# Grouped-query attention: Exp over three PSUM banks, one bank each for VectorE's scores and for outputs, chains of three cells

## The chip, the core and the metric

The kernel runs on one core of one Trainium2 chip. The metric is device time in microseconds. The core has these engines: TensorE (PE in the profile; PEld is its weight load), VectorE (DVE), ScalarE (ACT), GpSimd (POOL) and SyncE (SP, here only a DMA queue). Each engine runs its own instruction stream in order, and semaphores make one stream wait for another. TensorE writes its results into PSUM, which has eight banks of 128 partitions by 512 fp32 numbers.

## The reference

```
batch, n_q_heads, n_kv_heads, seq, head_dim = (8, 8, 2, 1024, 64)
...
scale = 1.0 / np.sqrt(head_dim)
for g in range(n_kv_heads):
    ...
    scores = scale * np.matmul(q_group, k_group.transpose(0, 1, 3, 2))
    scores_max = np.max(scores, axis=-1, keepdims=True)
    attn = np.exp(scores - scores_max)
    attn = attn / (np.sum(attn, axis=-1, keepdims=True) + 1e-08)
    output[:, q_start:q_end, :, :] = np.matmul(attn, v_group)
```

The inputs are fp32, normal numbers times 0.1. Four query heads share one key and value head. The kernel computes in bf16 and leaves the maximum out.

## The kernel before

**Jobs and cells.** A job is one batch, one query head and one half of its 1024 queries: 8 x 8 x 2 = 128 jobs. A job has eight cells, one for each 128 keys. A cell is one score matmul: 128 keys on the partitions by 512 queries, in one PSUM bank (`score`, L466). So there are 1024 cells.

**Two ways to the exponential.** An A cell goes to ScalarE: cells are gathered in a PSUM tile of two banks (`aps`, two such tiles), and one ACTIVATE with Exp (`exps`, L477) turns the whole tile into bf16 in a ring in SBUF (`p_ring`). A D cell goes to VectorE: its score lies in one of two single banks (`dps`), and VectorE makes from it the bits of a bf16 power of two (`exp_bits`, L491, called p1 below). Ten such cells form a group `pd`, and a chain of four instructions over the group corrects the mantissa: "and" (L512, VectorE), "line" (L516, GpSimd, the linear factor), "prod" (L525, VectorE) and "add" (L527, VectorE).

**Outputs.** For each cell, four small matmuls (`output_mms`, L538, called a PV below) multiply the exponentials by V, which has a column of ones, so the sum of the exponentials comes with it. The eight PVs of one job add up in one PSUM bank (`ops`; there are two). Then `normalise` takes the reciprocal of the sum (L551) and multiplies (L554), both on VectorE, into a staging tile, from where a DMA writes the result. The first PV of a job that takes an output bank (it "opens" the bank) must wait until the job before in that bank has been normalised.

**PSUM.** 2 tiles x 2 banks for Exp, 2 banks for VectorE's scores, 2 for outputs: eight in all.

**The order of the work** is written by a planner, `make_plan`. It steps through the kernel with a clock for each engine and a cost for each operation, takes at each step the operation that could start soonest, and notes its time. The notes, sorted by time, are the order in which the instructions are issued on every engine (`tc.manual_schedule`, L617); semaphores still enforce the real dependences. The planner's costs and limits are the constants of L34 to L42. An output bank is chosen in an event of its own:

```
            at = max(pe, FIRST_PV, min(obank_free), at)
...
        elif kind == "open":
            o = first_free(obank_free)
            obank[arg] = o
            obank_free[o] = INF
```

and the PVs of the job are noted afterwards at `max(pe, FIRST_PV, ready...)` (L94).

**Data.** Q and K are cast to bf16 through a DRAM scratch by GpSimd's DMA queue (L323) and brought back transposed by SyncE's (L335); V comes by GpSimd's queue (L356). A cast is made to wait for the latest score matmul planned before it (L329), as a brake. GpSimd's DMA issues stand in the same stream as its "line" instructions; `at_pool` moves an issue behind a "line" if it would fall shortly before it.

Of the kernel before, what the change touches and what calls it, by code (L numbers as in the profile page):

```python
# [11 lines left out]

CURVE_A, CURVE_B = 0.32988085, -0.33401025

A_CELLS, D_BANKS, O_BANKS = (2, 2), 2, 2
GROUP, PARTS = 10, 2
CHAIN = ("and", "line", "prod", "add")
ON_POOL = ("line",)

def part(step, m):  # L20

    n = step[-1]
    return slice(0, m) if not n.isdigit() else slice(m * int(n) // PARTS, m * (int(n) + 1) // PARTS)


def make_plan(nj, nkc):
# [6 lines left out]

    QK, PV, P1, NORM = 0.216, 0.1225, 0.603, 0.555  # L34
    EXP = (0.05, 0.4268)
    FOUR, TWO, POOL_ONE = (0.09, 0.133), (0.05, 0.27), (0.25, 0.43)
    COST = {"and": FOUR, "line": POOL_ONE, "prod": TWO, "add": TWO}
    FROM_PE, FROM_PV, FROM_ACT, FROM_DVE, FROM_POOL = 0.21, 0.16, 0.165, 0.10, 0.15
    LIVE_A, LIVE_D, PENDING, PER_JOB, LEAD, RAMP, AHEAD, FIRST_PV = 28, 5, 16, 2, 6, 6, 0.0, 2.0
    INF = 1e9  # L40
    AHEAD_D, EXTRA, LAST = 0, 0, 6
    FIRST_TURN, FIRST_LOAD, EACH_LOAD = 2.4, 4.5, 4.2  # L42
    ops = []
    pe = act = dve = pool = two_end = 0.0
# [7 lines left out]
    p1q, chainq, normq, cur = [], [], [], []  # L52
# [10 lines left out]
    def first_free(slots):  # L63
        return min(range(len(slots)), key=lambda s: slots[s])


    while normed < nj:
# [46 lines left out]
        if kind == "qk":  # L114
            t = best[4]
            pe = t + QK
            j = job_d if arg else job_a
            cell = j * nkc + todo[j].pop(0)
            if not arg:
                if open_a is None:  # L120
                    slot = first_free(a_free)
                    a_id += 1
                    live["A"] += 1
                    open_a = {"slot": slot, "t": a_free[slot], "cells": []}
                    a_free[slot] = INF
                o = open_a
                ops.append((t, "qk", cell, "A", a_id, o["slot"], len(o["cells"])))
                o["cells"].append(cell)
                home[cell] = ("A", a_id)
                if len(o["cells"]) == A_CELLS[o["slot"]] or not any(todo[job_a:]):  # L130
                    act = max(act, pe + FROM_PE)
                    ops.append((act, "exp", a_id, tuple(o["cells"])))
                    act += EXP[0] + EXP[1] * len(o["cells"])
                    a_free[o["slot"]] = act + FROM_ACT
                    uses[("A", a_id)] = len(o["cells"])
                    for x in o["cells"]:
                        ready[x] = act + FROM_ACT
                    open_a = None
            else:
                taken[j] += 1  # L140
                k = first_free(bank)
                bank[k] = INF
                pending += 1
                ops.append((t, "qk", cell, "D", k, 0, 0))
                p1q.append((pe + FROM_PE, cell, k))
# [4 lines that stand above are left out]
            open_jobs.append(arg)  # L150
            rem[arg] = list(range(nkc))
            next_job += 1
        elif kind == "pv":
            s, c = arg
            cell = s * nkc + c
            opens = len(rem[s]) == nkc
            rem[s].remove(c)
            done = not rem[s]
            ops.append((t, "pv", s, cell, opens, done, obank[s]))
            pe = t + PV  # L160
            h = home[cell]
            uses[h] -= 1
            if not uses[h]:
                live[h[0]] -= 1
            if done:
                open_jobs.remove(s)
                normq.append((pe + FROM_PV, s))
        elif kind == "norm":
            s = normq.pop(0)[1]
            ops.append((t, "norm", s))  # L170
            dve = t + NORM
            obank_free[obank[s]] = dve + FROM_DVE
            normed += 1
        elif kind == "p1":
            _, cell, k = p1q.pop(0)
            if not cur:
                d_id += 1
                live["D"] += 1
            ops.append((t, "p1", cell, k, d_id, len(cur)))
            dve = t + P1  # L180
            bank[k] = dve + FROM_DVE
            cur.append(cell)
            home[cell] = ("D", d_id)
            if len(cur) == GROUP:
                chainq.append((dve, d_id, cur, 0))
                cur = []
        elif kind == "flush":
            chainq.append((dve, d_id, cur, 0))
            cur = []
        else:  # L190
            _, g, cells, step = chainq.pop(arg)
            ops.append((t, "chain", g, len(cells), CHAIN[step]))
            name = CHAIN[step]
            fixed, each = COST[name.rstrip("0123456789")]
            end = t + fixed + each * len(cells[part(name, len(cells))])
            if name in ON_POOL:
                pool = end
            else:
                dve = two_end = end
            if step + 1 < len(CHAIN):  # L200
                at = end
                if (name in ON_POOL) != (CHAIN[step + 1] in ON_POOL):
                    at += FROM_POOL if name in ON_POOL else FROM_DVE
                chainq.insert(arg, (at, g, cells, step + 1))
            else:
                pending -= len(cells)
                uses[("D", g)] = len(cells)
                for x in cells:
                    ready[x] = dve + FROM_DVE
# [4 lines left out]
def kernel(  # L214
# [8 lines left out]
    FP32 = mybir.dt.float32  # L223
    BF16 = mybir.dt.bfloat16
# [12 lines left out]
    QBS = 512  # L237
    HALF = S // 2
# [3 lines left out]
    PIECE = 512  # L242
    WARM = 30
    CAST_GAP = 3.0
    P_TILES = 28
    POOL_DMA = 1.0
    OBSERVE = 26
    scale = 1.0 / math.sqrt(D)
    bits_scale = 128.0 * scale * math.log2(math.e)
    bits_bias = 128.0 * 127.0  # L250
# [13 lines left out]
    const_pool = ctx.enter_context(tc.tile_pool(name="constp", bufs=1))  # L264
# [3 lines left out]
    first_pool = ctx.enter_context(tc.tile_pool(name="firstp", bufs=1))  # L268
    qT_pool = ctx.enter_context(tc.tile_pool(name="qTpool", bufs=10))
    kT_pool = ctx.enter_context(tc.tile_pool(name="kTpool", bufs=4))  # L270
    pd_pool = ctx.enter_context(tc.tile_pool(name="pdpool", bufs=5))
    tmp_pool = ctx.enter_context(tc.tile_pool(name="tmppool", bufs=2))
    ostage_pool = ctx.enter_context(tc.tile_pool(name="ostage", bufs=6))
    recip_pool = ctx.enter_context(tc.tile_pool(name="recip", bufs=10))
# [1 line left out]
    def psum_pools(name, n):  # L276
        return [
            ctx.enter_context(
                tc.tile_pool(name=f"{name}{i}", bufs=1, space=bass.MemoryType.PSUM)
            )  # L280
            for i in range(n)
        ]

    apools, dbanks, obanks = psum_pools("aps", 2), psum_pools("dps", 2), psum_pools("ops", 2)

    p_ring = const_pool.tile([128, P_TILES, 2, QBS], BF16)
    blank = const_pool.tile([128, 128], BF16)
    nc.vector.memset(blank, 1.0)  # L288
    ident = const_pool.tile([128, 128], BF16)
# [75 lines left out]
    def first_loads():  # L365
# [5 lines left out]

        hk = first_pool.tile([128, NHC, 3, D], BF16, name="hk")

        tk = [
            dbanks[0].tile([128, HALF], BF16, name="dps0"),
            apools[1].tile([128, HALF], BF16, name="aps1"),
        ]
        lo, hi = slice(0, D), slice(D, 2 * D)

        def turn_k(w, half, bank):  # L380
# [21 lines left out]
        for two in range(2):  # L402
            place_v(0, 0, two)

        warm = obanks[1].tile([128, 128], FP32, name="ops1")

        def keep_warm(n):
            for _ in range(n):
# [1 line left out]
            return mm.ins  # L410

        hq = first_pool.tile([128, NHC, 2 * D], BF16, name="hq")
        tq = [
            dbanks[1].tile([128, HALF], BF16, name="dps1"),
            obanks[0].tile([128, HALF], BF16, name="ops0"),
        ]
        qT[(0, 0)] = qT_pool.tile([128, HALF], BF16, name="qT")
        last_score[0] = keep_warm(WARM)
        for n, half in enumerate(halves):
# [30 lines left out]
    psum = {}  # L450
# [6 lines left out]
    def score(cell, kind, n, slot, col):  # L457
        b, h, side = jobs[cell // NKC]
        c = cell % NKC
        if kind == "A":  # L460
            if col == 0:
                psum[("A", n)] = apools[slot].tile([128, 2, QBS], FP32, name=f"aps{slot}")
            dst = psum[("A", n)][:, col, :]
        else:
            dst = psum[cell] = dbanks[n].tile([128, QBS], FP32, name=f"dps{n}")
        last_score[0] = nc.tensor.matmul(  # L466
            dst,
            lhsT=ksets[b % 2][:, h // HPG, side, c * 128 : (c + 1) * 128],
            rhs=qT[(b, h)],
            start=True,  # L470
            stop=True,
        ).ins

    def exps(n, cells):
        pt = p_ring[:, n % P_TILES]
        m = len(cells)
# [4 lines left out]
        exp_ins.append(act.ins)  # L481
        if n >= P_TILES and (n - P_TILES) % OBSERVE == 0:
            seen = exp_ins[n - P_TILES + OBSERVE - 1]
            tc.add_manual_dep(act.ins, seen.name, SYNC, reason="ring")
# [101 lines left out]
    for b in range(B):  # L586
        for h in range(H):
# [3 lines left out]
            spare = min(1.0, max(0.0, th - 12.0) / 60.0)  # L591
# [59 lines left out]
```

The softmax here doesn't subtract the row's maximum and nothing guards it: scores larger than these inputs give would overflow.

## Time and profile before

| | |
|---|---|
| median of 3 runs | 385.43 us (385.39 to 386.04) |
| the profiled execution | 385.81 us |
| its span, first to last instruction | 384.0 us |
| TensorE clock granted | 1.00 of full speed nearly throughout, 0.998 in the mean |
| ACTIVATE with Exp | 404, of two banks each |
| cells on ScalarE / VectorE | 808 / 216 |
| chains | 21 of ten cells, one of six |

An instruction's time in the profile runs from its start to its end; on VectorE and ScalarE the next one may start a little before the end of the last. So the cost of an instruction in a full engine is best read from start to start, and an engine that reads as 100% busy may still lose some hundredths of a microsecond at each instruction. In the table of waits each line has the engine and line that waited, who released it, the total wait in us, how often, and the longest. In the timeline each line has the start, the length, the engine, the source line, the operation, out<-in and how many were merged; an idle time before it and its releaser may stand in brackets.

### The profile page before, as it was taken

What the parts mean: (1) busy time and instruction counts of PE and PEld (TensorE: products, weight loads), DVE (VectorE), ACT (ScalarE), POOL (GpSimd) and SP (SyncE); (2) the same over time, 40 slices, a digit from 0 to 9 for tenths busy, and PEclk for the clock granted to TensorE, in tenths of its full rate; (3) what the DMA queues carried; (4) which work ended last, traced back from release to release, by engine and by line L of the source; (5) the groups of instructions that cost most, each with busy time, mean ns of one, the idle gap of its engine ahead of it and who ended that gap; (6) DMA issues with size and microseconds to landing.
All of it is one profiled execution on the core that took longest, in us unless ns stands there. A gap on an engine that the chain in (4) does not pass through costs nothing.

```text
span 384.0 us, 12026 instructions
## 1 busy us (share of the span) xinstructions
PE 365.6 (95%) x5172; PEld 233.6 (61%) x5172; DVE 353.8 (92%) x548; ACT 374.6 (98%) x409; POOL 174.4 (45%) x147
## 2 busy tenths in 40 slices
PE   8879898999999999999999999999999999998995
PEld 7425464666666666666666666666666666564664
DVE  4779998999999999999999999999999999989982
ACT  5999999999999999999999999999999999999995
POOL 5584535718244371563718245271643627040420
PEclk9999999999999999999999999999999999999999
DMA  8988988697756848585676759468675765711213
GB/s 137 135 152 135 130 154 124 129 147 140 113 109 132 140 103 139 101 156 103 139 131 120 130 106 152 96 126 137 105 124 123 138 102 119 126 56 29 57 56 84
DMA packets 102485, 45.48 MB, mean 118 GB/s; under 512 B 63792, under 2 KB 100976, under 8 KB 101184
## 3 DMA queue, kind: packets, MB, share of 16 engines
q1 hardware_dynamic: 82096, 31.21, 36.1%
q0 software_dynamic: 19712, 13.18, 32.3%
q8 instruction: 40, 0.66, 0.7%
q10 hardware_dynamic: 624, 0.33, 0.3%
q14 instruction: 13, 0.11, 0.1%
HBM read 25.17 MB, written 27.00 MB: 136 GB/s over the span
## 4 chain that ended last, share of the span: by engine, by line
ACT 86%; PE 10%; DVE 2%; issue 1%
ACT p_ring L477 86%; PE aps L466 4%; PE ops L538 4%; PE ops L409 1%; PE dps L466 1%; DVE pd L527 1%; DVE ost L554 0%; DVE y L525 0%; DVE z L512 0%; DVE rec L551 0%; PE dps L382 0%; PE dps L428 0%; PE ops L428 0%; PE aps L382 0%; DVE blank L288 0%
## 5 line engine op out<-in xcount | busy, mean ns | idle before, releaser
L477 ACT ACTIVATE p_ring<-aps 128x1024 bf16<-128x1024 f32 x404 | 371.8, 1067 | 1.4 <-PE aps L466 1.2
L466 PE MATMUL aps<-qT,kset 128*128 128x512 bf16 x808 | 239.9, 378 | 13.0 <-ACT p_ring L477 12.4
L538 PEld LDWEIGHTS <-p_ring 128*128 128x128 bf16 x3232 | 140.1, 98 | 64.0
L538 PE MATMUL ops<-vset,p_ring 128*128 128x65 bf16 x3232 | 154.6, 194 | 0.0
L491 DVE TENSOR_SCALAR pd<-dps 128x512 uint16<-128x512 f32 x216 | 138.6, 683 | 7.0 <-PE dps L466 6.7
L516 POOL TENSOR_SCALAR y<-z 128x5120 f16<-128x5120 uint16 (+1 forms) x22 | 96.4, 4383 | 70.0 <-DVE rec L551 48.7
L466 PEld LDWEIGHTS <-kset 128*128 128x128 bf16 x1024 | 79.7, 97 | 56.4 <-issue 25.8
L323 POOL DMA_DIRECT2D scr_q<-in_q_dram x63 | 39.1, 621 | 83.5 <-PE dps L466 44.3
L466 PE MATMUL dps<-qT,kset 128*128 128x512 bf16 x216 | 76.4, 379 | 0.0
L525 DVE TENSOR_TENSOR y<-z,y 128x5120 f16<-128x5120 uint16 (+1 forms) x22 | 61.0, 2772 | 1.1 <-POOL y L516 1.1
L527 DVE TENSOR_TENSOR pd<-pd,y 128x5120 uint16<-128x5120 uint16 (+1 forms) x22 | 60.9, 2769 | 0.1
L554 DVE TENSOR_TENSOR ost<-ops,rec 128x256 f32<-128x256 f32 x128 | 54.3, 425 | 4.4
L538 PEld LDWEIGHTS <-pd 128*128 128x128 bf16 x864 | 42.8, 98 | 24.7 <-DVE ost L554 2.2
L538 PE MATMUL ops<-vset,pd 128*128 128x65 bf16 x864 | 52.2, 194 | 0.3
L512 DVE TENSOR_SCALAR z<-pd 128x5120 uint16<-128x5120 uint16 (+1 forms) x22 | 32.3, 1467 | 0.5
L551 DVE RECIPROCAL rec<-ops 128x4 f32<-128x4 f32 x128 | 22.6, 176 | 9.6 <-PE ops L538 8.2
L323 POOL DMA_DIRECT2D scr_k<-in_k_dram x15 | 9.8, 656 | 39.9 <-PE aps L466 33.0
L356 POOL DMA_DIRECT2D vset<-in_v_dram x32 | 24.9, 784 | 0.0
L409 PE MATMUL ops<-blank 128*128 128x128 bf16 x40 | 5.3, 313 | 1.1 <-DVE blank L288 1.1
L409 PEld LDWEIGHTS <-blank 128*128 128x128 bf16 x40 | 4.4, 149 | 1.1 <-DVE blank L288 1.1
L363 POOL DMA_DIRECT2D kset<-kset x6 | 4.1, 684 | 0.0
L420 ACT ACT_TABLE_LOAD x1 | 1.3, 1283 | 1.8 <-issue 1.8
(23 smaller groups left out, 10.2 us busy)
## 6 DMA issues: line engine op xcount, KB each, us to landing
out_dram<-ost SPq DMA_DIRECT2D x63, 256.0 KB, 2.9
scr_q<-in_q_dram POOLq DMA_DIRECT2D x63, 128.0 KB, 3.5
kset<-kT SPq DMA_DIRECT2D x60, 64.0 KB, 3.1
vset<-in_v_dram POOLq DMA_DIRECT2D x32, 64.0 KB, 3.9
scr_k<-in_k_dram POOLq DMA_DIRECT2D x15, 128.0 KB, 3.7
qT<-scr_q SPq DMA_TRANSPOSE x63, 3.5
kset<-kset POOLq DMA_DIRECT2D x6, 128.0 KB, 4.3
fq<-in_q_dram ACTq DMA_DIRECT2D x2, 128.0 KB, 3.3
```

Of the source, the lines that this page charges most:

```text
L323: dma = nc.gpsimd.dma_start(out=scr.rearrange("(p f) -> p f", f=1024), in_=src.rearrange("(p s) d -> p (s d)", s=1024 // D),)
L356: nc.gpsimd.dma_start(out=vsets[b % 2][:, g, two * NHC : (two + 1) * NHC, 0:D], in_=v[b, g].rearrange("(c p two) d -> two p c d", p=128, t ...
L466: last_score[0] = nc.tensor.matmul(dst, lhsT=ksets[b % 2][:, h // HPG, side, c * 128 : (c + 1) * 128], rhs=qT[(b, h)], start=True, stop=Tr ...
L477: act = nc.scalar.activation(out=pt[:, 0:m], in_=psum.pop(("A", n))[:, 0:m], func=AF.Exp, scale=scale)
L491: nc.vector.tensor_scalar(out=groups[g][:, slot], in0=psum.pop(cell), scalar1=bits_scale, scalar2=bits_bias, op0=ALU.mult, op1=ALU.add,)
L512: eng.tensor_scalar(out=z, in0=pd, scalar1=0x7F, scalar2=None, op0=ALU.bitwise_and)
L516: eng.tensor_scalar(out=y, in0=z, scalar1=CURVE_A / 128.0, scalar2=CURVE_B, op0=ALU.mult, op1=ALU.add,)
L525: eng.tensor_tensor(out=y, in0=z, in1=y, op=ALU.mult)
L527: eng.tensor_tensor(out=pd, in0=pd, in1=y, op=ALU.add)
L538: nc.tensor.matmul(ops_of[s][:, qs, :], lhsT=p_of[cell][:, qs * 128 : (qs + 1) * 128], rhs=vsets[b % 2][:, h // HPG, c, :], start=opens an ...
L551: nc.vector.reciprocal(out=rec, in_=o[:, :, D])
L554: nc.vector.tensor_tensor(out=stage[(b, h)][:, :, side, :], in0=o[:, :, 0:D], in1=rec.unsqueeze(2).to_broadcast([128, NQS, D]), op=ALU.mult,)
```

## The change

The Exp tiles have three banks instead of two, and there are still two of them: six banks. VectorE's scores have one bank instead of two, and so have the outputs. A chain covers three cells instead of ten. Its "line" stays on GpSimd. The planner's constants change with it. The group tiles `pd` grow in number from 5 to 8, and the ring holds 18 tiles of three cells instead of 28 of two. The first loads use other banks as scratch. The operations that are computed stay the same.

```diff
-A_CELLS, D_BANKS, O_BANKS = (2, 2), 2, 2
-GROUP, PARTS = 10, 2
+A_CELLS, D_BANKS, O_BANKS = (3, 3), 1, 1
+GROUP, PARTS = 3, 2
...
-    FOUR, TWO, POOL_ONE = (0.09, 0.133), (0.05, 0.27), (0.25, 0.43)
+    FOUR, TWO, POOL_ONE = (0.20, 0.133), (0.05, 0.27), (0.25, 0.417)
...
-    FROM_PE, FROM_PV, FROM_ACT, FROM_DVE, FROM_POOL = 0.21, 0.16, 0.165, 0.10, 0.15
-    LIVE_A, LIVE_D, PENDING, PER_JOB, LEAD, RAMP, AHEAD, FIRST_PV = 28, 5, 16, 2, 6, 6, 0.0, 2.0
+    FROM_PE, FROM_PV, FROM_ACT, FROM_DVE, FROM_POOL = 0.21, 0.20, 0.165, 0.135, 0.06
+    LIVE_A, LIVE_D, PENDING, PER_JOB, LEAD, RAMP, AHEAD, FIRST_PV = 18, 8, 6, 2, 2, 6, 0, 2.0
...
-    AHEAD_D, EXTRA, LAST = 0, 0, 6
+    AHEAD_D, EXTRA, LAST = 0.1, 0, 6
...
-                chainq.append((dve, d_id, cur, 0))
+                chainq.append((dve + 0.11, d_id, cur, 0))
...
-    P_TILES = 28
+    P_TILES = 18
...
-    OBSERVE = 26
+    OBSERVE = 16
...
-    pd_pool = ctx.enter_context(tc.tile_pool(name="pdpool", bufs=5))
+    pd_pool = ctx.enter_context(tc.tile_pool(name="pdpool", bufs=8))
...
-    apools, dbanks, obanks = psum_pools("aps", 2), psum_pools("dps", 2), psum_pools("ops", 2)
-
-    p_ring = const_pool.tile([128, P_TILES, 2, QBS], BF16)
+    apools = psum_pools("aps", len(A_CELLS))
+    dbanks, obanks = psum_pools("dps", D_BANKS), psum_pools("ops", O_BANKS)
+
+    p_ring = const_pool.tile([128, P_TILES, max(A_CELLS), QBS], BF16)
...
-        tk = [
-            dbanks[0].tile([128, HALF], BF16, name="dps0"),
-            apools[1].tile([128, HALF], BF16, name="aps1"),
-        ]
+        spare = apools[1].tile([128, A_CELLS[1], 2 * QBS], BF16, name="aps1")
+        tk = [dbanks[0].tile([128, HALF], BF16, name="dps0"), spare[:, 0, :HALF]]
...
-        warm = obanks[1].tile([128, 128], FP32, name="ops1")
+        warm = apools[0].tile([128, 128], FP32, name="aps0")
...
-        tq = [
-            dbanks[1].tile([128, HALF], BF16, name="dps1"),
-            obanks[0].tile([128, HALF], BF16, name="ops0"),
-        ]
+        tq = [spare[:, 1, :HALF], obanks[0].tile([128, HALF], BF16, name="ops0")]
...
-                psum[("A", n)] = apools[slot].tile([128, 2, QBS], FP32, name=f"aps{slot}")
+                psum[("A", n)] = apools[slot].tile(
+                    [128, A_CELLS[slot], QBS], FP32, name=f"aps{slot}"
+                )
```

The order in which the changed kernel issues its instructions can be read without running it. It has 273 ACTIVATEs of three banks and one of one bank (820 A cells), 204 p1 (204 D cells), and 68 chains of three cells. On VectorE the cycle most often repeated is: p1, and, p1, normalise, p1, prod, add, normalise.

More of the change, by code (lines that the diff above doesn't have):

```diff
@@ L184, in make_plan @@
             if len(cur) == GROUP:
-                chainq.append((dve, d_id, cur, 0))
+                chainq.append((dve + 0.11, d_id, cur, 0))
                 cur = []
         elif kind == "flush":
-            chainq.append((dve, d_id, cur, 0))
+            chainq.append((dve + 0.11, d_id, cur, 0))
             cur = []
```

## The prediction

> **What bounds the kernel now.** I read the page first: busy time, then the chain of waits, then the costliest groups.
>
> ```profile
> PE 365.6 (95%) x5172; PEld 233.6 (61%) x5172; DVE 353.8 (92%) x548; ACT 374.6 (98%) x409; POOL 174.4 (45%) x147
> ...
> ACT 86%; PE 10%; DVE 2%; issue 1%
> ...
> L477 ACT ACTIVATE p_ring<-aps 128x1024 bf16<-128x1024 f32 x404 | 371.8, 1067 | 1.4 <-PE aps L466 1.2
> ```
>
> ScalarE carries the end (86% of the chain is Exp), with TensorE and VectorE close behind it. Its 100% hides small losses: by the timeline an Exp starts 0.90 us after the last at best, and the 404 take 372 us from 7.40 to 379.43, which is 0.92 each. So 404 x 0.903 = 364.8 is work and some 7 us are waits of hundredths, for the two-bank tiles. The table of waits shows the same from TensorE's side, and how rarely the output bank matters with two of them:
>
> ```profile
> PE aps L466 <- ACT p_ring L477: 12.4, 40, 0.3
> ...
> PEld L538 <- DVE ost L554: 2.2, 5, 0.6
> ```
>
> One of those five waits, in the timeline at 30 us, gives the price of a normalise for the PV behind it: reciprocal at 30.47, multiply at 30.68, ended at 31.11, next PV at 31.16. So the bank comes back **0.69 us** after the reciprocal starts, and TensorE started no other matmul meanwhile.
>
> ```profile
> 30.47 0.18 DVE L551 RECIPROCAL rec<-ops 128x4 f32<-128x4 f32 x1
> 30.68 0.42 DVE L554 TENSOR_TENSOR ost<-ops,rec 128x256 f32<-128x256 f32 x1
> ...
> 30.51 0.59 PE L466 MATMUL aps<-qT,kset 128*128 128x512 bf16 x2
> 31.16 0.42 PE L538 MATMUL ops<-vset,pd 128*128 128x65 bf16 x8
> ...
> 31.16 0.30 PEld L538 LDWEIGHTS <-pd 128*128 128x128 bf16 x8 [0.55 <-DVE ost L554]
> ```
>
> The score bank's round trip, from the same view: p1 starts at 203.79, the next score in its bank at 204.53 (0.74 later); a score that starts at 7.63 is read by p1 at 8.05 (0.42).
>
> ```profile
> 203.79 0.68 DVE L491 TENSOR_SCALAR pd<-dps 128x512 uint16<-128x512 f32 x1
> ...
> 204.53 0.38 PE L466 MATMUL dps<-qT,kset 128*128 128x512 bf16 x1
> ```
>
> VectorE's costs, start to start, for chains of ten cells and the one of six:
>
> ```profile
> 201.83 1.49 DVE L512 TENSOR_SCALAR z<-pd 128x5120 uint16<-128x5120 uint16 x1
> 203.24 0.17 DVE L551 RECIPROCAL rec<-ops 128x4 f32<-128x4 f32 x1
> ...
> 366.53 0.95 DVE L512 TENSOR_SCALAR z<-pd 128x3072 uint16<-128x3072 uint16 x1
> 367.40 0.18 DVE L551 RECIPROCAL rec<-ops 128x4 f32<-128x4 f32 x1
> ...
> 370.35 1.76 DVE L525 TENSOR_TENSOR y<-z,y 128x3072 f16<-128x3072 uint16 x1
> 372.03 0.18 DVE L551 RECIPROCAL rec<-ops 128x4 f32<-128x4 f32 x1
> ```
>
> "and": 1.41 for ten, 0.87 for six, so 0.135 a cell and 0.06 fixed: 0.465 for three. "prod": 2.74 (207.95 to 210.69) and 1.68, so 0.265 and 0.09: 0.885 for three. "add": 2.74 and 1.66, so 0.86. Where add follows prod at once it starts 2.85 after it (24.28, 27.13), 0.11 more: 0.99. p1 costs 0.60, normalise 0.55 (203.24 to 203.79).
>
> **What the Trainium skill says.** "Perfetto Trace Analysis", section Matmuls: independent matmul groups should rotate through PSUM banks so that reading one out lies beside the next group's matmuls. The trace agrees: with two output banks, 2.2 us of waits in 128 jobs. "TensorE: Matmul & The Clock Gate", section Step-by-step: only weight loads are pulled ahead, "The MATMULs themselves stay in program order". The gap before 31.16 agrees. So a PV that waits holds every score behind it. The same page, section "A second HAM failure mode": short idle times between groups of matmuls can lower the granted clock. Here the clock is 0.998, so the trace does not show it; it serves as a rival. For a price: "ScalarE: Activation LUTs", section "What ACT_TABLE_LOAD costs", gives 0.833 ns an element, so a third bank adds an estimated 512 x 0.833 = 0.427 to 0.903: **1.330** for a three-bank Exp. The trace has only one length; 0.45 at most (half of 0.903, nothing fixed) to 0.41 at least bounds the whole at +7 and -5 us.
>
> **The change part by part.**
> 1. Exp: 273 x 1.330 + 0.48 = 363.6 of issue, 1.2 less than before (131 instructions fewer, twelve A cells more). A two-bank tile has little slack: 1.07 (Exp) + 0.215 (second score) + 0.42 = 1.70 of 1.81. A three-bank one has 1.50 + 0.43 + 0.42 = 2.35 of 2.66, 0.31. So most of the 7 us of small waits could go.
> 2. VectorE: chains 22 x 6.9 less the short one = 149 before; 68 x (0.465 + 0.99 + 0.86) = 157 after; p1 twelve fewer, -7. About +1, beside Exp.
> 3. GpSimd: "line" of three takes 4.46 - 7 x 0.427 = 1.47 (slope from 4.46 and 2.75), in all 100 us of an engine that is half idle. From "and" to "prod": 0.55 + 0.12 + 1.47 + 0.03 = 2.17. Its DMA issues stand behind a line and have over 2 us to the next. Nothing.
> 4. Start: VectorE's first score is now first on TensorE, in the bank that held the turned K, so it waits for the copy at L391 (6.40 + 0.42). First Exp at about 7.9 instead of 7.40.
> 5. One score bank and one output bank. Here I follow the order of issue through the cycle that fills 49 of the 68 chains. Jobs X, Y, Z; time 0 is the reciprocal of X, right behind an add. TensorE: six PVs of Y (the first opens the bank), two A scores, D score b, an A score, two PVs that end Y, two A, D score c, one A, then Z opens. VectorE: normalise X, p1 a, and, p1 b, normalise Y, p1 c, prod, add, normalise Z.
>    - Y's first PV: 0.69 (the one bank). Six PVs are 24 matmuls at 0.031: 0.74. Two A scores at 0.215: 0.43. D score b at 1.86, p1 b at 1.86 + 0.42 = 2.28. VectorE alone would be there at 0.55 + 0.60 + 0.465 = 1.61, so it stands idle for 0.67.
>    - Normalise Y at 2.88; p1 c at 3.43 (by VectorE 2.88 + 0.55, by the bank 2.28 + 0.74 + 0.42, equal); prod at 4.04 (line done at 1.15 + 2.17 = 3.32, in time); add 5.03; normalise Z at **5.89**.
>
>    The cycle closes at 5.89 although no engine has that much work: VectorE 5.22, ScalarE 4 x 1.330 = 5.32, TensorE 15 x 0.215 + 16 x 0.124 = 5.21. It is a loop: normalise, output bank, PVs, score, p1, normalise, p1, chain, normalise. With two output banks the PVs of Y would not wait. The planner misses it: the event that takes a bank knows when it is free, but the PVs are noted at TensorE's own clock, so scores meant for ScalarE and VectorE are placed behind a PV that stalls.
>    - So Exp loses 5.89 - 5.32 = 0.57 in each such cycle: 49 x 0.57 = 27.9. The other 19 chains have more scores between jobs. Following one such stretch the same way, three chains (one of the common kind, two others) take 16.49 against 3 x 5.32 = 15.96, so only the common one loses; the one after it has five PVs in front and loses 0.12 less (-0.7 over six places). 27.2.
>
> Sum: 7.9 + 363.6 + 27.2 + 1.5 for the first chains and small waits (I take 1.5 from 0 to 4) + 4.7 from the last Exp's issue to the span's end, as now (379.43 to 384.0, and 0.1 of overlap) = 404.9. The profiled execution has 1.8 outside its span and lies 0.4 above the median: **406.3**.
>
> **Rivals.**
> - *The loop is looser.* If a normalise finds its PVs earlier than I think, or slack carried from the other chains covers 0.3 of each 0.57, 49 x 0.27 = 13: 392. For it: the bank waits are rare before. Against: that was with two banks.
> - *Faster.* The PVs do not stall VectorE's score, the cycle stays at 5.32, and point 1 is all that counts: 406.3 - 27.2 - 1.5 = 378, up to 384 with some waits left. It decides if the PV gets its bank within about 0.12 us of the reciprocal (0.69 - 0.57). The trace speaks against it.
> - *Heavier.* The idle times lower TensorE's clock: of the loop 0.74 + 0.43 + 0.42 is TensorE's, 1.2 more per cycle at half speed; in a tenth of the cycles 6 us, in a fifth 12: 412 to 418. Against: it stays 88% busy (5.21 of 5.89).
> - *VectorE as the bound* by its shorter instructions: 5.22 plus a few hundredths of bank waits is about Exp's 5.32, so some 386. Point 2 gives it little.
>
> **How the numbers follow.** Forecast as worked out, 398 to 412: 0.68. Looser or VectorE-bound, 386 to 398: 0.13. Heavier: 0.11. Faster: 0.08. The range 393 to 415 holds the first, most of the third and half of the second. About 0.2% (0.8 us) is what the measurement can tell from no change: faster 0.08, same 0.02, slower 0.90.
>
> **What would show it.** Right: Exp idle of some 0.5 us every fourth or fifth Exp, released by TensorE's scores; PV weight loads waiting on L554 of around 0.4 us, dozens of times; p1 waiting for a score; VectorE near 89% busy or less, a cycle of 5.9 in its timeline. Wrong: ScalarE still at 98% (then the bank is not waited for), waits of prod on GpSimd, or a clock under 0.95.

## The result, and the profile after

The changed kernel takes **410.16 us** (median of 4 runs, 409.48 to 410.39), the kernel before 385.47 us: a ratio of 1.0634, 95% interval 1.0616 to 1.0653. The profiled execution took 410.39 us, its span is 408.6 us.

First the page of the changed kernel: busy times, the chain that ended last, and the groups that answer to those of before.

```profile
PE 370.7 (91%) x5088; PEld 222.2 (54%) x5172; DVE 354.1 (87%) x674; ACT 375.5 (92%) x279; POOL 168.9 (41%) x193
...
DVE 51%; PE 24%; ACT 16%; DMA 4%; issue 4%
...
L475 ACT ACTIVATE p_ring<-aps 128x1536 bf16<-128x1536 f32 x274 | 372.8, 1464 | 23.0 <-PE aps L464 22.8
L489 DVE TENSOR_SCALAR pd<-dps 128x512 uint16<-128x512 f32 x204 | 140.1, 687 | 36.3 <-PE dps L464 35.6
```

No engine has much more work than before: VectorE is busy for 354.1 us against 353.8, ScalarE for 375.5 against 374.6, TensorE for 370.7 against 365.6. The span is 24.6 us longer all the same, so the time went into waits. The chain says whose: Exp carried 86% of it, and now 16%; it runs through VectorE and TensorE instead. The groups show p1 idle for 35.6 us until a score came (6.7 before), and Exp for 22.8 us (1.2 before).

The table of waits of the changed kernel (engine, line, who released it; us in total, times, longest) names the other end:

```profile
PEld L536 <- DVE ost L552: 71.0, 113, 1.2
...
DVE pd L489 <- PE dps L464: 35.6, 62, 1.2
...
PE aps L464 <- ACT p_ring L475: 4.2, 9, 0.5
```

TensorE's weight loads for PVs wait for the normalise 113 times, 71 us in all; before it was 5 times and 2.2 us. The last line fell as well: TensorE waited 12.4 us for an Exp tile before, now 4.2. That fits the longer slack of three-bank tiles, but does not show it: e6 below, with two-bank tiles, has 4.5.

One common cycle in the timeline, VectorE first, then TensorE:

```profile
183.37 0.17 DVE L549 RECIPROCAL rec<-ops 128x4 f32<-128x4 f32 x1
183.58 0.42 DVE L552 TENSOR_TENSOR ost<-ops,rec 128x256 f32<-128x256 f32 x1
183.92 0.68 DVE L489 TENSOR_SCALAR pd<-dps 128x512 uint16<-128x512 f32 x1
184.52 0.55 DVE L510 TENSOR_SCALAR z<-pd 128x1536 uint16<-128x1536 uint16 x1
185.65 0.69 DVE L489 TENSOR_SCALAR pd<-dps 128x512 uint16<-128x512 f32 x1 [0.59 <-PE dps L464]
```

```profile
184.06 0.30 PE L536 MATMUL ops<-vset,pd 128*128 128x65 bf16 x4 [0.35 <-DVE ost L552]
184.19 0.78 PE L536 MATMUL ops<-vset,p_ring 128*128 128x65 bf16 x20
184.80 0.60 PE L464 MATMUL aps<-qT,kset 128*128 128x512 bf16 x2
185.24 0.38 PE L464 MATMUL dps<-qT,kset 128*128 128x512 bf16 x1
```

Read from the reciprocal at 183.37: the PV that opens the bank starts 0.69 us later. With it come six PVs, then two scores for ScalarE; VectorE's score b starts at 1.87, p1 b at 2.28. VectorE had ended "and" at 185.07 (184.52 + 0.55) and stood idle for 0.59 us until p1 b began. From one "and" to the next it is 5.908 us in the median of the 55 cycles with two normalises in the common order.

### The profile page after: what moved, and what is told of

Read it like the earlier page. It is cut to its first block, busy times and chain, and to the rows that moved or that the text cites. A ratio compares the mean times of both kernels' runs of the same rounds, so it can differ in the third digit from the quotient of the medians.

```text
span 408.6 us, 11995 instructions
## 1 busy us (share of the span) xinstructions
PE 370.7 (91%) x5088; PEld 222.2 (54%) x5172; DVE 354.1 (87%) x674; ACT 375.5 (92%) x279; POOL 168.9 (41%) x193
## 4 chain that ended last, share of the span: by engine, by line
DVE 51%; PE 24%; ACT 16%; DMA 4%; issue 4%
ACT p_ring L475 16%; DVE pd L489 15%; PE ops L536 12%; DVE ost L552 11%; DVE y L523 11%; DVE pd L525 10%; PE aps L464 7%; PE dps L464 4%; DVE rec L549 4%; DMA out_dram<-ost 3%; PE aps L408 1%; DMA kset<-kset 1%; DVE z L510 0%; PE aps L381 0%; PE aps L424 0%
## 5 line engine op out<-in xcount | busy, mean ns | idle before, releaser
L475 ACT ACTIVATE p_ring<-aps 128x1536 bf16<-128x1536 f32 x274 | 372.8, 1464 | 23.0 <-PE aps L464 22.8
L464 PE MATMUL aps<-qT,kset 128*128 128x512 bf16 x736 | 231.2, 379 | 6.6 <-ACT p_ring L475 4.2
L489 DVE TENSOR_SCALAR pd<-dps 128x512 uint16<-128x512 f32 x204 | 140.1, 687 | 36.3 <-PE dps L464 35.6
L514 POOL TENSOR_SCALAR y<-z 128x1536 f16<-128x1536 uint16 x68 | 99.5, 1463 | 163.3 <-DVE z L510 162.3
L536 PEld LDWEIGHTS <-p_ring 128*128 128x128 bf16 x3280 | 131.8, 97 | 38.9 <-DVE ost L552 2.6
L536 PEld LDWEIGHTS <-pd 128*128 128x128 bf16 x816 | 33.9, 97 | 74.9 <-DVE ost L552 68.4
L525 DVE TENSOR_TENSOR pd<-pd,y 128x1536 uint16<-128x1536 uint16 x68 | 65.0, 956 | 2.0
L523 DVE TENSOR_TENSOR y<-z,y 128x1536 f16<-128x1536 uint16 x68 | 64.5, 948 | 0.9 <-POOL y L514 0.9
L324 POOL DMA_DIRECT2D scr_q<-in_q_dram x63 | 33.7, 534 | 52.2 <-PE aps L464 38.4
L510 DVE TENSOR_SCALAR z<-pd 128x1536 uint16<-128x1536 uint16 x68 | 37.4, 550 | 0.0
L408 PE MATMUL aps<-blank 128*128 128x128 bf16 x40 | 5.2, 312 | 1.1 <-DVE blank L289 1.1
```

What stands on the lines that cost most here:

```text
L324: dma = nc.gpsimd.dma_start(out=scr.rearrange("(p f) -> p f", f=1024), in_=src.rearrange("(p s) d -> p (s d)", s=1024 // D),)
L464: last_score[0] = nc.tensor.matmul(dst, lhsT=ksets[b % 2][:, h // HPG, side, c * 128 : (c + 1) * 128], rhs=qT[(b, h)], start=True, stop=Tr ...
L475: act = nc.scalar.activation(out=pt[:, 0:m], in_=psum.pop(("A", n))[:, 0:m], func=AF.Exp, scale=scale)
L489: nc.vector.tensor_scalar(out=groups[g][:, slot], in0=psum.pop(cell), scalar1=bits_scale, scalar2=bits_bias, op0=ALU.mult, op1=ALU.add,)
L510: eng.tensor_scalar(out=z, in0=pd, scalar1=0x7F, scalar2=None, op0=ALU.bitwise_and)
L514: eng.tensor_scalar(out=y, in0=z, scalar1=CURVE_A / 128.0, scalar2=CURVE_B, op0=ALU.mult, op1=ALU.add,)
```

## The experiments

All are timed against the kernel before on the same chip. Those that change the kernel of after keep its order unless the text says otherwise.

**e3 and e4: less and more of a normalise.** One takes the reciprocal out, the other issues the multiply twice.

```diff
-        nc.vector.reciprocal(out=rec, in_=o[:, :, D])
...
+        for _ in range(2):
             nc.vector.tensor_tensor(out=stage[(b, h)][:, :, side, :], ...)
```

> The changed kernel without the reciprocal: the multiply takes a constant, so the division by the sum is left out. A normalise is 0.21 us shorter. Theory (loop): only the first of the two normalises of a cycle counts, because p1 c then waits for its score bank: the cycle goes from 5.91 to about 5.70, 43 x 0.21 = 9, some 401 us. Rival (VectorE's sum of work bounds): 128 x 0.21 = 27, some 383 us. Rival (TensorE or ScalarE bound, normalise beside them): 410.

> The changed kernel with the multiply of each normalise issued twice, 0.34 us more per job. VectorE stands idle for 0.67 us of each common cycle, as much as two more multiplies take. Theory (loop): nothing of it is absorbed, both count: the cycle grows by 0.68 and the time by 50 x 0.68 to 128 x 0.34, 34 to 44, so 444 to 454 us. Rival (the idle time is free, the bound lies elsewhere): 410 to 415 us.

Measured: 396.84 us without the reciprocal (ratio to before 1.0294, 1.0273 to 1.0314), 466.29 with two multiplies (1.2095, 1.2071 to 1.2120). The cycle was 5.67 and 6.81 us. Without the reciprocal VectorE has 0.42 us less per cycle, and the cycle lost 0.23: one of the two counts, as the loop has it, and 55 x 0.23 = 13 of the 13.3 us. I had counted 43 cycles; it is all 55 that shrink. e4 came out above the 444 to 454 us expected: the second multiply starts 0.46 us after the first and not 0.34, and the cycle grew by 0.905, about twice that. Nothing was absorbed by VectorE's 0.59 us of idle time. So these microseconds lie on the loop.

**e1, e5, e9, e10: the wait for the bank taken away.** If the normalise reads a constant, no PV has to wait for it.

```diff
-        nc.vector.reciprocal(out=rec, in_=o[:, :, D])
+        nc.vector.reciprocal(out=rec, in_=other[:, :, D])
...
-            in0=o[:, :, 0:D],
+            in0=other[:, :, 0:D],
```

> The changed kernel in its own order, but the normalise reads a constant tile in SBUF in place of the output bank, so no PV waits for a normalise and no normalise for a PV; the outputs' division is left out of the computation this way, its two instructions stay. Theory (the loop through the one output bank): the common cycle falls from 5.91 us to ScalarE's four Exp, about 5.32, so 410 - 43 x 0.59 = 385, and less at the end where outputs queue: 380 to 386. Rival (the one score bank, or the short chains, make VectorE late by themselves): the cycle stays near 5.9 and the time at 400 or more.

Measured: **412.79 us**, and the cycle again 5.91. That would have felled the theory, had the timeline not shown another cycle of the same length:

```profile
179.71 0.17 DVE L551 RECIPROCAL rec<-other 128x4 f32<-128x4 f32 x1
179.91 0.42 DVE L554 TENSOR_TENSOR ost<-other,rec 128x256 f32<-128x256 f32 x1
180.25 0.68 DVE L491 TENSOR_SCALAR pd<-dps 128x512 uint16<-128x512 f32 x1
180.85 0.55 DVE L512 TENSOR_SCALAR z<-pd 128x1536 uint16<-128x1536 uint16 x1
181.44 0.69 DVE L491 TENSOR_SCALAR pd<-dps 128x512 uint16<-128x512 f32 x1
182.05 0.17 DVE L551 RECIPROCAL rec<-other 128x4 f32<-128x4 f32 x1
182.25 0.99 DVE L554 TENSOR_TENSOR ost<-other,rec 128x256 f32<-128x256 f32 x1
183.16 0.68 DVE L491 TENSOR_SCALAR pd<-dps 128x512 uint16<-128x512 f32 x1
```

```profile
181.50 1.46 POOL L516 TENSOR_SCALAR y<-z 128x1536 f16<-128x1536 uint16 x1 [2.03 <-DVE z L512]
```

VectorE has no gap of note in this cycle (388.8 us busy of 411.0 in all), and p1 b comes at 181.44, 1.73 after the reciprocal, as a free bank would have it. But the second multiply of the cycle takes 0.99 us in place of 0.42. It now reads both inputs from SBUF while GpSimd's line runs (181.50 to 182.96). The Trainium skill, "GPSIMD Engine Reference", section Key points, says that the two engines share their SBUF interfaces and contend when VectorE has two SBUF inputs or runs in a 2-port mode. The trace agrees: all 60 multiplies that overlap a line are longer (0.82 to 1.72 us), the other 68 keep 0.42. It also shows the form: each of the 60 ends 0.27 to 0.28 us after the line's end, whenever it started. So the multiply waits for the line. The edit had given back, by accident, what it took away. e5 takes an instruction with one strided tensor input.

> As e1, but the normalise's second instruction is one that reads a single strided constant from SBUF, since in e1 the multiply with two SBUF inputs took 0.99 us instead of 0.42 wherever GpSimd's line ran beside it. The normalisation is left out of the computation; two instructions of about the same length stand in its place; no PV waits for them. Theory (loop through the one output bank): the first PV of the opened job then waits for the add before it only, 0.14 us after the reciprocal's start instead of 0.69, and the cycle goes from 5.91 to 5.35: 410 - 50 x 0.56 = 382 to 386. Rival (the one score bank or the short chains are the limit): 400 or more.

Measured: 400.43 us (1.0387, 1.0369 to 1.0406), cycle 5.71. The one-input form was held up as well: the 60 that overlap a line end 0.15 us after it.

```profile
180.35 0.35 DVE L554 TENSOR_SCALAR ost<-other,rec 128x256 f32<-128x256 f32 x1
...
182.70 0.79 DVE L554 TENSOR_SCALAR ost<-other,rec 128x256 f32<-128x256 f32 x1
```

```profile
181.87 1.46 POOL L516 TENSOR_SCALAR y<-z 128x1536 f16<-128x1536 uint16 x1 [1.03 <-DVE z L512]
```

Both times lie where the rival was expected, but with a new wait in the place of the old one neither run separates the theories. So GpSimd's line was shortened too, from 1.46 to 0.26 us, with a control that shortens the line alone:

```diff
-                out=y,
-                in0=z,
+                out=y[:, :, 0:32],
+                in0=z[:, :, 0:32],
```

> Control for e10: the changed kernel in its own order, but GpSimd's line computes 32 of the 512 columns of each cell and the rest of y stays zero, so most of the linear factor is left out. Theory (loop through the output bank): the line had 0.7 us to spare before prod and lies beside a wait, so the cycle stays at 5.9 and the time at 408 to 411. Rival (the detour over GpSimd in each short chain is the limit): below 400.

> e5 and e9 together: no PV waits for a normalise (the normalisation is left out), and the line is short (most of the linear factor is left out), so nothing on GpSimd runs beside VectorE's SBUF operands, which took 0.79 instead of 0.35 us there in e5. Theory: the output bank's wait is now the only thing missing, and the cycle falls from 5.91 to about 5.35, ScalarE's 5.32 within reach: 380 to 388. Rival (the single score bank or the three-cell chains make VectorE late): 398 or more.

Measured: the control **411.0 us** (1.0653, 1.0632 to 1.0675), cycle 5.91, nothing gained; with the bank free as well **382.84 us** (0.9938, 0.9917 to 0.9960), cycle 5.38. VectorE and TensorE of e10:

```profile
177.77 0.17 DVE L554 RECIPROCAL rec<-other 128x4 f32<-128x4 f32 x1
177.97 0.35 DVE L557 TENSOR_SCALAR ost<-other,rec 128x256 f32<-128x256 f32 x1
178.24 0.68 DVE L494 TENSOR_SCALAR pd<-dps 128x512 uint16<-128x512 f32 x1
178.84 0.55 DVE L515 TENSOR_SCALAR z<-pd 128x1536 uint16<-128x1536 uint16 x1
179.50 0.69 DVE L494 TENSOR_SCALAR pd<-dps 128x512 uint16<-128x512 f32 x1
```

```profile
177.91 0.42 PE L541 MATMUL ops<-vset,pd 128*128 128x65 bf16 x8
...
179.09 0.38 PE L469 MATMUL dps<-qT,kset 128*128 128x512 bf16 x1
```

The PV starts 0.14 us after the reciprocal, p1 b at 1.73 instead of 2.28. With one score bank, short chains and three-bank tiles all in place, 28 us go when the wait for the output bank goes, 25 of them between the first and the last Exp and 3 behind the last; ScalarE is back at 98%. This is what shows the cause. Two other things went with it, both too small to be the whole. The instruction in the normalise's place is 0.07 us shorter than the multiply: 128 x 0.07 = 9 us at the very most, and by the measure of e3 (13.3 us for 0.21 each) an estimated 4. And the normalise no longer waits for its own PVs, which was 4.4 us in e9.

**e2: VectorE's scores moved forward** on TensorE in the common cycles, score b behind five PVs, score c before the last scores of an Exp tile.

```diff
+        new = p[:5] + d[:1] + p[5:] + a[:2] + d[1:] + a[2:]
```

> The changed kernel with the same banks, chains and VectorE order, but in the 49 common cycles TensorE gets VectorE's score b after five PVs of the newly opened job, before two A scores, and score c before the last A scores. Theory: p1 b can start at 0.69 + 0.62 + 0.42 = 1.73 instead of 2.28 after the reciprocal, and the loop closes at 5.35 to 5.42: 410 - 43 x 0.5 = 386 to 390. Rival (the output bank's wait is the whole loss, wherever the scores stand): as long as PVs wait for the one bank, 405 to 410. Rival (one score bank is the limit): p1 b cannot come earlier, 408 to 410.

Measured: 426.82 us (1.1072, 1.1045 to 1.1100), slower than the changed kernel. A miss. Its table of waits:

```profile
ACT p_ring L498 <- PE aps L487: 39.0, 51, 2.6
...
DVE rec L572 <- PE ops L559: 35.5, 52, 1.4
...
PE aps L487 <- ACT p_ring L498: 24.2, 60, 0.5
```

In the changed kernel the last two are 3.9 and 4.2 us. Score b did what it was moved for: p1 b starts 1.74 us after the reciprocal, in the median of the 49 cycles. The cycle still went to 6.16. By the order, score c ahead of the last A score makes that tile's Exp late, TensorE then stands before that tile, and the PVs behind it, which the next normalise needs, come late in turn. I had followed the loop over VectorE and left out the one over the Exp tiles. That reading comes from the waits; no run took it apart.

**e8: a planner that knows when the bank is free,** with limits chosen for it.

```diff
-                at = max(pe, FIRST_PV, ready.get(s * nkc + c, INF))
+                at = max(pe, FIRST_PV, bank_at[s], ready.get(s * nkc + c, INF))
...
+            bank_at[arg] = obank_free[o]
```

> The changed kernel's banks and chains, but a planner in which a PV that opens a bank is noted no earlier than the bank is free, with limits chosen for it (lead of scores -0.1, four jobs ahead, ten cells pending). Theory: the bank's turnaround cannot be hidden wholly, but scores no longer stand behind a stalled PV: VectorE's cells fall to 164, ScalarE has 286 tiles of 1.33 = 380 us and becomes the bound again: 394 to 402. Rival (the single bank costs the same in any order): 408 or more.

Measured: 398.47 us (1.0336, 1.0320 to 1.0352). ScalarE is 98% busy with 287 Exp, VectorE 77%. So an order that is honest about the bank gets 12 us back on the same banks, with fewer cells for VectorE (164 instead of 204); it does not get back to before. Three things changed with it (rule, limits, split of the cells), so this is no measure of the rule alone.

**e6, e7, e11: other splits of the banks** (e6 and e7 use seven of the eight), with the chains of three and the costs of after, Exp tiles of two banks, and the planner free to order anew. The edit is that of e6; e7 has two score banks and one output bank, e11 two and two.

```diff
-A_CELLS, D_BANKS, O_BANKS = (3, 3), 1, 1
+A_CELLS, D_BANKS, O_BANKS = (2, 2), 1, 2
-    AHEAD_D, EXTRA, LAST = 0.1, 0, 6
+    AHEAD_D, EXTRA, LAST = 0, 0, 6
```

> The changed kernel's chains of three, its constants (the lead of VectorE's scores over ScalarE's at 0 as before) and its one score bank, but Exp tiles of two banks again and two output banks; the planner orders anew. Theory: the loop is gone, what is left is two-bank Exp tiles with the old small waits and chains of three: 384 to 394. Rival (one score bank, or chains of three): 400 or more.

> The counterpart of e6: Exp tiles of two banks, chains of three, two score banks and one output bank; the planner orders anew. Theory: the output bank's loop stays: 398 to 412, and clearly above e6. Rival (the score bank is the limit): clearly below e6, 385 to 392.

> The changed kernel's chains of three and constants (the lead of VectorE's scores at 0) on the banks of before: Exp tiles of two banks, two score banks, two output banks; the planner orders anew and gives VectorE 185 cells. Theory: no loop; ScalarE has 420 Exp at 0.92, 386 us, against 372 before, so 392 to 402, from the planner's split and not from waits for an output bank, which stay under 10 us. Rival (short chains cost as much as the change did): 408 or more.

Measured: two output banks and one score bank 396.06 us (1.0271, 1.0255 to 1.0286); one and two 420.48 (1.0905, 1.0885 to 1.0925); two and two 408.97 (1.0601, 1.0583 to 1.0618). e6 is 24 us faster than e7, so a second bank served the outputs better than VectorE's scores; in e7 the weight loads wait 36.9 us for the normalise. How much of the 24 us is the bank is not shown. The planner made another order for each, 7 of the 24 us lie behind the last Exp (11.5 us in e7, 4.1 in e6), and GpSimd's line holds up more instructions in e7. Both lie above what I expected, and e11 well above, where its rival (short chains cost as much) was expected. But e11 is no clean test of short chains either: its order lets chain instructions of one group run beside GpSimd's line of another.

```profile
198.59 0.95 DVE L523 TENSOR_TENSOR y<-z,y 128x1536 f16<-128x1536 uint16 x1
...
205.72 2.21 DVE L523 TENSOR_TENSOR y<-z,y 128x1536 f16<-128x1536 uint16 x1 [0.81 <-POOL y L514]
```

```profile
203.98 3.13 POOL L514 TENSOR_SCALAR y<-z 128x1536 f16<-128x1536 uint16 x2 [1.63 <-DVE z L510]
```

The prod of 2.21 us would take 0.95. In e11 36 chain instructions are held up so, 41 us longer together than usual; in e7 34 (21 us), in e6 13 (9 us), in the changed kernel and e8 none. How much of that reached the end is not shown. What chains of three cost by themselves on the old banks stays open; in the order of the changed kernel they cost no wait (e9, e10).

## Why the prediction was right

The direction, the mechanism and the size held; it came out 3.9 us short of the measured median.

- *Exp.* 1.330 us per three-bank tile was the estimate from the slope in the Trainium skill, "ScalarE: Activation LUTs", section What ACT_TABLE_LOAD costs; the trace has 1.330 from start to start where nothing waits. The first Exp started at 7.95 (7.9 foreseen). The fewer waits for tiles came too, though e6 has as few without three-bank tiles.
- *VectorE and GpSimd beside it.* VectorE's busy time grew by 0.3 us (about 1 foreseen). prod waited 0.9 us in all for GpSimd, and shortening the line changed nothing (e9).
- *The loop.* 5.89 us foreseen, 5.908 measured; p1 b at 2.28 both times. Shown as the cause by e10 with its control e9, and by the doses e3 and e4.
- *The sum.* Exp ran 393.4 us from its first to its last start, against 273 x 1.330 = 363.1: 30.3 us of waits, where the forecast had 27.2 and 1.5. That is 1.6 us more: the loop is 0.02 longer, the three chains where the order changes take 16.63 where I took 16.49, and the cycle after them 5.86 where I took 5.77. Within the three the loss lies elsewhere than I said: they take 5.91, 5.18 and 5.54 us, so a chain not of the common kind loses too, and the common one behind it loses less.
- *The term that was off most* is the end. I took 4.7 us from the last Exp's issue to the span's end, as before. It took 6.8 (from 401.8 to 408.6). With one output bank the last jobs go through it one after the other, each a full turn of 1.9 us:

```profile
401.30 0.17 DVE L549 RECIPROCAL rec<-ops 128x4 f32<-128x4 f32 x1
...
403.19 0.18 DVE L549 RECIPROCAL rec<-ops 128x4 f32<-128x4 f32 x1 [1.25 <-PE ops L536]
...
405.08 0.18 DVE L549 RECIPROCAL rec<-ops 128x4 f32<-128x4 f32 x1 [1.25 <-PE ops L536]
```

  e7, also with one output bank, ends in the same steps of 1.9 us. I had priced the single bank in the steady state and not in the tail.
- *Rivals.* The clock stayed at 1.00, so the heavier case did not occur; the faster one would have needed the bank within 0.12 us, and it came after 0.69. The loop was not looser: slack carried over shortens only the first two cycles of a stretch (5.54 and 5.86). VectorE was no bound by its work, at 87% busy. The remark that the planner misses the bank is half of it: a better order helps (e8), a wrong one hurts more (e2), and the wait itself is the single bank.

## What to carry to other kernels

When a buffer goes from two to one, follow one whole turn through every in-order engine, from its release to the next release, and compare the turn with the work of the busiest engine: here 5.9 against 5.3 us, which no busy share shows. A gain elsewhere (TensorE's waits for Exp tiles fell from 12.4 to 4.2 us) did not pay here for a bank taken from the consumer whose release holds the queue of the engine that feeds all others. And in an experiment that removes a wait, check that each instruction kept its length: e1 met the old cycle time to the hundredth for another reason.

## What the runs showed of the hardware

- Where a VectorE instruction that takes its tensors from SBUF was held up by GpSimd's tensor_scalar, it ended a fixed time after that one's end, whenever it had started: the multiply with two fp32 inputs 0.27 to 0.28 us after (e1, all 60 that overlap; 0.82 to 1.72 us long, alone 0.42), a tensor_scalar with one strided fp32 input 0.15 us after (e5, all 60), prod and add 0.80 to 0.82, "and" 0.42 (e11, 36 instructions). That is a wait and not a lower rate. The reciprocal of four SBUF numbers kept its 0.17 us beside the line (e1), and p1, which reads PSUM, its 0.69.
- Two VectorE instructions in a row cost 0.11 us more where the second reads the first's result: add starts 0.98 us after prod, while an independent instruction follows prod after 0.87. The second of two equal multiplies, which writes the same tile as the first, starts 0.46 us after it, against the 0.34 after which another instruction follows.
